# A two-layer GLA and MLA trunk on Trainium2: first products from a transposed copy of x, its norm applied afterwards, c_q in 512-column blocks

## The chip, the cores and the metric

The kernel runs on one core of a Trainium2 chip. The metric is the device time of one execution in microseconds (us). The engines are TensorE (PE in the profile; its weight loads are PEld), VectorE (DVE), ScalarE (ACT), GpSimd (POOL) and SyncE (SP), which issues most of the DMA transfers. Each runs its own instructions in a fixed order and waits on semaphores for the others.

## The reference

One sequence of 512 rows of width 2048 goes through two layers; each takes an RMS norm of x, a token mixer, an RMS norm of the mixer's output, and adds it to x. All in float32. Cut to what matters here:

```python
def rms_norm(x, g, eps=1e-6):
    return x * rsqrt(mean(x * x, -1) + eps) * g

for i in range(2):
    h = rms_norm(x, g_pre)
    y = gla_mixer(h, ...) if i == 0 else mla_mixer(h, ...)
    x = x + rms_norm(y, g_post)

def gla_mixer(h, ...):            # 4 heads, 256 wide in q and k, 512 in v
    q, k, v, gate, gk_low = split(h @ w_in)      # 1024, 1024, 2048, 2048, 16
    log_a = log_sigmoid(gk_low @ w_gk2 + b_gk) / 16
    ...                           # chunked linear attention with decays from log_a
    return (rms_norm(o, g_onorm) * silu(gate)) @ w_out

def mla_mixer(h, ...):            # 16 heads
    c_q, c_kv, k_rope, gate = split(h @ w_in)    # 512, 512, 64, 2048
    q  = rms_norm(c_q,  g_qa)  @ w_qb
    kv = rms_norm(c_kv, g_kva) @ w_kvb
    ...                           # causal softmax attention
    return (o * silu(gate)) @ w_out
```

## The kernel before

**Products.** Every large product is made of three matmuls (`mm3`, L123): each factor is split into a high part, which the fast matmul format holds exactly, and the rest (`act_hi`, `act_lo`; `w_hi`, `w_lo`), and hi x hi, hi x lo and lo x hi are added up in a PSUM bank. `act_hi` and `act_lo` hold the normed x transposed, as 16 slices k of 128 rows by 512 columns. Weights come in chunks: SyncE loads half a megabyte (`chunk_load`, three buffers), ScalarE writes the high part and VectorE the rest (`chunk_split`, four buffers). Where a norm's gain g belongs in front of the product, `chunk_split` multiplies it into the weights, one k at a time (L118, L119); without a gain it takes the whole chunk in one copy and one subtraction (L110, L111). `block_s` makes products with the sequence on the rows of the result (four row tiles s, four banks), `block_t` with the sequence on the columns.

**The start** (`start`, L224). x is loaded by rows, 1 MB for each row tile s, the first in four pieces. For each s ScalarE sums the squares, `rstd_of` makes the factor, and `rows_to_act` (L324) scales the rows, has PE transpose them in 16 blocks of 128x128 (L333, four to a bank) and splits the result into `act_hi` and `act_lo`. In between PE makes the products of v for head 0, columns 0 to 255, with 4 k to a chunk. The gains of the norm before layer 0 arrive as rows and are transposed by PE (`gain_t`), other gains likewise later (`gcols` in `constants`). Then `gla` makes columns 256 to 511 of v (L346), the 16 columns of gk_low with 48 columns of weights (`gk_low`), and for each head the q/k block, the gate block, v, scores and values. Evacuations: `v_evac` splits v, `qk_block` multiplies q and k by their decays, `silu` makes the gate.

**Between the layers** (`between`, L611, called by `out_proj` for each s when the last columns are done). VectorE adds the residual to `yo` in four passes (L619), ScalarE sums squares, SyncE stores the new x (`x1d`), and `rows_to_act` norms and transposes it for layer 1, as at the start. `cq_ahead` (L688) has loaded and split the weights of columns 0 to 255 of c_q for 14 of the 16 k before. `mla` then makes, s by s, columns 0 to 255 of c_q from these, and columns 256 to 511 by `block_s`, 4 k to a chunk; `latent_evac` norms the rows of c_q, and `latent_end` transposes them (`lat_t`).

**What sets the order.** The code is written once in program order; a scheduler then fixes the order of instructions on each engine, and in that order each engine waits. PE's order thus interleaves transposes with products. Transposes use two PSUM banks (`pt`), products four, and two are left for scores.

Of the kernel before, what the change touches and what calls it, by code (L numbers as in the profile page):

```python
# [70 lines left out]
class Trunk:  # L71
# [152 lines left out]
    def start(self):  # L224

        nc, a, cp = self.nc, self.a, self.cp
        xs = a["x"][0]
        xt = [self.slot(f"g{s}", [P, D], F32, f"x{s}") for s in range(ST)]
        rows = self.tmp([KT, P], F32, "gain_rows")
# [1 line left out]
        for g in range(4):
            c = slice(g * 512, (g + 1) * 512)
            nc.sync.dma_start(xt[0][:, c], xs[0:P, c])
            if g == 0:
                nc.scalar.dma_start(cf, a["consts"])
                nc.scalar.dma_start(rows, a["l0_pre_norm"].rearrange("(r c) -> r c", c=P))
# [5 lines left out]
        nc.tensor.transpose(pt[:, 0:KT], rows, self.ident[0:KT, 0:KT])
        self.g_in = cp.tile([P, KT], F32, name="g_in0")
        nc.vector.tensor_copy(self.g_in, pt[:, 0:KT])
        w = a["l0_gla_w_in"]
        load = lambda i: self.chunk_load(w, 4 * i, 4, [(GV0, 256)])
        raws = [load(0)]
        nc.sync.dma_start(xt[1], xs[P:2 * P, :])
        raws.append(load(1))
        nc.sync.dma_start(xt[2], xs[2 * P:3 * P, :])  # L250
        raws.append(load(2))
        ws = []
        self.v_ps = [self.acc(f"v_acc{s}", s == 3) for s in range(ST)]
        for s in range(ST):
            parts = self.st.tile([P, 4], F32, tag="parts", name="parts", bufs=2)
            for g in range(4):
                self.sumsq(xt[s][:, g * 512:(g + 1) * 512], parts[:, g:g + 1])
            rstd = self.rstd_of(self.total(parts, "x_ssq"), D, "x_rstd")
            self.rows_to_act(s, xt[s], rstd)
            for i in range(4):  # L260
                if s == 0:
                    if i == 3:
                        raws.append(load(3))
                        nc.sync.dma_start(xt[3], xs[3 * P:4 * P, :])
                    ws.append(self.chunk_split(raws[i], 4 * i, self.g_in, hi_on=nc.vector if i % 2 else None))
                self.part_s(s, 4 * i, ws[i], self.v_ps, slice(0, 256), self.act_hi, self.act_lo, KT)

    def constants(self):
# [21 lines left out]
        pt = self.pst.tile([P, 512], F32, tag="pt", name="gcols")  # L290
        nc.tensor.transpose(pt[:, 0:NROWS], rows[0:NROWS, :], self.ident[0:NROWS, 0:NROWS])
        self.gcol = cp.tile([P, NROWS], F32, name="gcol")
        nc.vector.tensor_copy(self.gcol, pt[:, 0:NROWS])
        with self.tc.issue_after(self.last_norm.ins):
# [635 lines left out]
```

## Time and profile before

| | us |
|---|---|
| median of 3 runs | 1505.87 (1505.53 to 1507.59) |
| the profiled execution | 1507.5 |
| its span in the profile | 1505.7 |
| PE busy in it | 1485.8 (99%) |
| DVE, ACT busy | 742.5 (49%), 657.1 (44%) |
| DMA, mean | 100 GB/s |

The span runs from the first instruction to the last; times in timelines are counted from its start. PE's busy time is pipelined: two matmuls overlap, so what one costs in a row of them is the distance of their starts, not the duration beside it. PE is busy in all 40 slices of the page but for the first and the last; so the order of its instructions and what it waits for there are what a reader has to look at.

### The profile page before, as it was taken

Reading aid. Unit: us, or ns where it says so; the run is one execution under the profiler, and the core shown is the slowest. Engines: PE = TensorE matmul, PEld = TensorE weight load, DVE = VectorE, ACT = ScalarE, POOL = GpSimd, SP = SyncE. Lnnn points to the kernel's source line nnn. Section 1 sums busy time; section 2 is a strip of 40 time slices with the busy share of each in tenths; the row PEclk is TensorE's granted clock in tenths of the full one; section 3 lists DMA queues with packets and bytes.
Section 4 is the critical chain, followed back from the end, with each engine's and each line's share of the span. In section 5 each row is a group of like instructions: output and inputs, shape, how many; then the busy total and the mean of one; then the engine's idle time right before and its main releaser. Section 6 shows DMA issues by size and latency. Waiting matters only on the chain.

```text
span 1505.7 us, 19208 instructions
## 1 busy us (share of the span) xinstructions
PE 1485.8 (99%) x7490; PEld 1266.6 (84%) x7490; DVE 742.5 (49%) x1337; ACT 657.1 (44%) x1250; POOL 35.0 (2%) x72
## 2 busy tenths in 40 slices
PE   7999999999999999999999999999999999999998
PEld 6988888888888888888889888888888899888886
DVE  6544653355436445434355443333577677853234
ACT  6542642254225424333244443344566667742221
POOL 2100000000000000100011000000000000000000
PEclk9999999999999999999999999999999999999999
DMA  6423223322331323434252333333222111234223
GB/s 222 122 71 98 71 87 95 101 82 80 90 110 57 98 84 119 134 111 134 91 188 92 101 98 98 98 99 91 74 74 74 50 50 55 83 126 168 98 91 119
DMA packets 113867, 149.91 MB, mean 100 GB/s; under 512 B 17580, under 2 KB 66976, under 8 KB 112368
## 3 DMA queue, kind: packets, MB, share of 16 engines
q1 hardware_dynamic: 110176, 136.86, 29.9%
q0 software_dynamic: 3424, 11.75, 2.4%
q8 instruction: 58, 0.95, 0.3%
q14 instruction: 33, 0.27, 0.1%
q10 hardware_dynamic: 176, 0.07, 0.0%
HBM read 140.08 MB, written 8.59 MB: 99 GB/s over the span
## 4 chain that ended last, share of the span: by engine, by line
PE 95%; DVE 2%; ACT 1%; DMA 1%; issue 0%; SPq 0%; DVEq 0%; ACTq 0%
PE acc L125 11%; PE acc L127 11%; PE acc L126 11%; PE yo_acc L125 8%; PE yo_acc L126 8%; PE yo_acc L127 8%; PE v_acc L127 5%; PE v_acc L125 5%; PE v_acc L126 5%; PE o_t L127 1%; PE o_t L126 1%; PE q_acc L127 1%; PE q_acc L126 1%; PE q_acc L125 1%; PE o_t L125 1%; PE pt L882 1%
## 5 line engine op out<-in xcount | busy, mean ns | idle before, releaser
L125 PE MATMUL acc<-act_hi,w_hi 128*128 128x512 f32 x768 | 299.7, 390 | 0.0
L126 PE MATMUL acc<-act_hi,w_lo 128*128 128x512 f32 x768 | 299.2, 390 | 0.0
L127 PE MATMUL acc<-act_lo,w_hi 128*128 128x512 f32 x768 | 298.9, 391 | 0.0
L119 DVE SCALAR_TENSOR_TENSOR w_lo<-w_raw,g_in,w_hi 128x512 fp32r<-128x512 f32 (+1 forms) x208 | 139.7, 707 | 206.7 <-ACT w_hi L118 206.6
L118 ACT ACTIVATE w_hi<-w_raw,g_in 128x512 fp32r<-128x512 f32 (+1 forms) x200 | 128.1, 689 | 242.9 <-PE acc L127 166.6
L127 PEld LDWEIGHTS acc<-act_lo,w_hi 128*128 128x128 f32 x768 | 144.2, 188 | 30.7 <-issue 0.7
L125 PEld LDWEIGHTS acc<-act_hi,w_hi 128*128 128x128 f32 x768 | 144.2, 188 | 30.4 <-issue 0.7
L126 PEld LDWEIGHTS acc<-act_hi,w_lo 128*128 128x128 f32 x768 | 144.3, 188 | 29.8
L111 DVE TENSOR_TENSOR w_lo<-w_raw,w_hi 128x1024 fp32r<-128x1024 f32 x64 | 78.4, 1225 | 166.7 <-ACT w_hi L110 166.6
L110 ACT CAST w_hi<-w_raw 128x1024 fp32r<-128x1024 f32 x64 | 67.3, 1051 | 168.4 <-PE yo_acc L126 156.8
L125 PE MATMUL yo_acc<-w_hi,act_hi 128*128 128x512 f32 x352 | 137.5, 391 | 0.0
L126 PE MATMUL yo_acc<-w_hi,act_lo 128*128 128x512 f32 x352 | 137.1, 390 | 0.0
L127 PE MATMUL yo_acc<-w_lo,act_hi 128*128 128x512 f32 x352 | 137.1, 391 | 0.0
L119 DVE SCALAR_TENSOR_TENSOR w_lo<-w_raw,gcol,w_hi 128x512 fp32r<-128x512 f32 (+1 forms) x98 | 64.6, 699 | 106.1 <-ACT w_hi L118 105.9
L126 PE MATMUL v_acc<-w_hi,act_lo 128*128 128x512 f32 (+1 forms) x320 | 112.2, 352 | 0.0
L118 ACT ACTIVATE w_hi<-w_raw,gcol 128x512 fp32r<-128x512 f32 (+1 forms) x98 | 61.4, 677 | 115.5 <-PE acc L127 83.8
L125 PE MATMUL v_acc<-w_hi,act_hi 128*128 128x512 f32 (+1 forms) x320 | 111.5, 351 | 0.2 <-ACT act_hi L174 0.2
L127 PE MATMUL v_acc<-w_lo,act_hi 128*128 128x512 f32 (+1 forms) x320 | 110.7, 350 | 0.0
L127 PEld LDWEIGHTS yo_acc<-w_lo,act_hi 128*128 128x128 f32 x352 | 66.1, 188 | 14.0 <-issue 0.2
L125 PEld LDWEIGHTS yo_acc<-w_hi,act_hi 128*128 128x128 f32 x352 | 66.1, 188 | 13.8 <-issue 0.2
L126 PEld LDWEIGHTS yo_acc<-w_hi,act_lo 128*128 128x128 f32 x352 | 66.1, 188 | 13.4
L125 PEld LDWEIGHTS v_acc<-w_hi,act_hi 128*128 128x128 f32 x320 | 61.4, 192 | 8.0 <-ACT act_hi L174 0.6
(300 smaller groups left out, 2688.9 us busy)
## 6 DMA issues: line engine op xcount, KB each, us to landing
w_raw<-in_l_gla_w_in_dram SPq DMA_DIRECT2D x64, 512.0 KB, 3.7
w_raw<-in_l_mla_w_in_dram SPq DMA_DIRECT2D x47, 512.0 KB, 3.7
w_raw<-in_l_gla_w_in_dram SPq DMA_DIRECT2D x64, 256.0 KB, 3.0
w_raw<-in_l_gla_w_out_dram SPq DMA_DIRECT2D x32, 512.0 KB, 3.7
w_raw<-in_l_mla_w_out_dram SPq DMA_DIRECT2D x32, 512.0 KB, 3.6
pw_raw<-in_l_mla_w_kvb_dram SPq DMA_DIRECT2D x64, 128.0 KB, 2.3
xo<-in_x_dram POOLq DMA_DIRECT2D x16, 256.0 KB, 6.0
x1d<-yo SPq DMA_DIRECT2D x4, 1024.0 KB, 5.8
```

The lines of the kernel that those rows point to most:

```text
L110: nc.scalar.copy(hi, raw)
L111: nc.vector.tensor_tensor(lo, raw, hi.bitcast(F32), ALU.subtract)
L118: nc.scalar.activation(hi[:, kk, :], raw[:, kk, :], AF.Copy, scale=g)
L119: nc.vector.scalar_tensor_tensor(lo[:, kk, :], raw[:, kk, :], g, hi[:, kk, :].bitcast(F32), ALU.mult, ALU.subtract)
L125: t.matmul(out, lh, rh, start=start, stop=False)
L126: t.matmul(out, ll, rh, start=False, stop=False)
L127: t.matmul(out, lh, rl, start=False, stop=stop)
L882: te.transpose(pt[:, o:o + P], probs[i][:, j * P:(j + 1) * P], self.ident)
```

## The change

- x is also given transposed by the host (`xt`), and all gains as columns of one table (`gains`, 52 columns; `gcol`). The two PE transposes of gains go.
- `start` loads x^T in slices k, two at a time, alternating with weight chunks of 2 k by 512 columns of v. `x_split` writes `act_hi` and `act_lo` of a slice from x^T times the gain of layer 0, without the norm's factor: the 64 transposes of x go. The v block of head 0 is made of 512 columns at once; its chunks need no gain.
- The squares of x are summed per slice on ScalarE (`x_sq`) and VectorE (`x_ssq`, 128x512); before the last two k, `x_norm` sums them over partitions by matmuls with ones and makes the factor twice: as a column for each s (`rcol`) and along the sequence on all partitions (`rrow`).
- The factor is applied to the products: `v_evac` scales by `rcol`; the q/k blocks, the gates and gk_low are multiplied by `rrow` on VectorE. Weights of layer 0 are split without a gain.
- The weights of gk_low are prepared inside the v loop (`gk_weights`).
- c_q is made of 512 columns: `cq_ahead` prepares 7 of 16 k by 512 columns, `mla` adds the eighth, and `block_s` makes k 8 to 15 for all 512 columns.

```diff
     def start(self):
...
+        xs = [self.slot(f"g{i}", [P, 4, S], F32, f"xt{i}") for i in range(4)]
+
+        def load_x(k0, nk):
+            nc.sync.dma_start(xs[k0 // 4][:, k0 % 4:k0 % 4 + nk, :],
+                              a["xt"][k0 * P:(k0 + nk) * P, :].rearrange("(k p) n -> p k n", p=P))
+
+        self.gcol = cp.tile([P, NCOLS], F32, name="gcol")
+        nc.scalar.dma_start(self.gcol, a["gains"])
+        load_x(0, 1)
+        raws = [self.wp.tile([P, 2, 512], F32, tag="raw", name="w_raw", bufs=3)]
+        for k in range(2):
+            nc.sync.dma_start(raws[0][:, k, :], w[k * P:(k + 1) * P, GV0:GV0 + 512])
+            if k == 0:
+                load_x(1, 1)
...
+        for k0 in range(0, KT, 2):
+            if k0:
+                load_x(k0, 2)
+                raws.append(self.chunk_load(w, k0, 2, [(GV0, 512)]))
+            x = xs[k0 // 4][:, k0 % 4:k0 % 4 + 2, :]
+            if k0:
+                self.x_split(k0, 2, x)
+                wt = self.chunk_split(raws[-1])
+            else:
...
+                for k in range(2):
+                    self.x_split(k, 1, x[:, k:k + 1, :])
+                    v.tensor_copy(hi[:, k, :], raws[0][:, k, :])
+                    v.tensor_tensor(lo[:, k, :], raws[0][:, k, :], hi[:, k, :].bitcast(F32), ALU.subtract)
...
+                    nc.scalar.activation(sq, x[:, i, :], AF.Square)
+                    v.tensor_tensor(ssq, ssq, sq, ALU.add)
+            if k0 == 10:
+                self.gk_weights()
+            if k0 + 2 == KT:
+                self.x_norm(ssq)
+            for s in range(ST):
+                if k0 + 2 == KT:
+                    with self.tc.issue_after(self.norm_mm.ins):
+                        self.part_s(s, k0, wt, ps, slice(0, 512), self.act_hi, self.act_lo, KT)
+                    self.v_evac(s, ps[s])
+                else:
+                    self.part_s(s, k0, wt, ps, slice(0, 512), self.act_hi, self.act_lo, KT)
+
+    def x_split(self, k0, nk, x):
...
+            self.nc.scalar.activation(self.act_hi[:, k, :], x[:, i, :], AF.Copy, scale=g)
+            self.nc.vector.scalar_tensor_tensor(self.act_lo[:, k, :], x[:, i, :], g,
+                                                self.act_hi[:, k, :].bitcast(F32),
+                                                ALU.mult, ALU.subtract)
+
+    def x_norm(self, ssq):
...
         for s in range(ST):
...
+            nc.tensor.matmul(pc[:, s:s + 1], ssq[:, s * P:(s + 1) * P], self.ones[:, 0:1],
+                             start=True, stop=True)
+        pn = self.pss.tile([P, 512], F32, tag="sc", name="x_norm")
+        self.norm_mm = nc.tensor.matmul(pn, self.ones, ssq, start=True, stop=True)
...
     def v_evac(self, s, ps):
-        self.split_from(ps, self.vh[s], self.vl[s])
+        r = self.rcol[:, s:s + 1]
+        self.last_evac = self.nc.scalar.activation(self.vh[s], ps, AF.Copy, scale=r)
+        self.nc.vector.scalar_tensor_tensor(self.vl[s], ps, r, self.vh[s].bitcast(F32),
+                                            ALU.mult, ALU.subtract)
...
         def evac(t, ps):
             d = t % 2
+            n = self.tmp([P, S], F32, "qk")
+            v.tensor_tensor(n, ps, self.rrow, ALU.mult)
...
-    def silu(self, out, ps):
+    def silu(self, out, ps, r=None):
...
+        if r is not None:
+            nc.vector.tensor_tensor(g, ps, r, ALU.mult)
+            ps = g
...
-        self.cq_w.append(self.chunk(w, KT - 2, 2, [(MQ0, 256)], self.g_in))
+        self.cq_w.append(self.chunk(w, KT // 2 - 1, 1, [(MQ0, 512)], self.g_in))
         for s in range(ST):
             for i, wt in enumerate(self.cq_w):
-                self.part_s(s, 2 * i, wt, ps, slice(0, 256), hi, lo, KT)
-        self.block_s(w, MQ0 + 256, 256, 256, ps, hi, lo, KT, evac=self.latent_evac, gain=self.g_in)
+                self.part_s(s, i, wt, ps, slice(0, 512), hi, lo, KT)
+        self.block_s(w, MQ0, 512, 0, ps, hi, lo, KT, evac=self.latent_evac, gain=self.g_in,
+                     ks=(KT // 2, KT))
...
-        for k0, nk in ((0, 4), (4, 4), (8, 4), (12, 2)):
-            raw = self.chunk_load(w, k0, nk, [(MQ0, 256)])
...
+        for k0, nk in ((0, 2), (2, 2), (4, 2), (6, 1)):
+            raw = self.chunk_load(w, k0, nk, [(MQ0, 512)])
```

How the scheduler's order moves is seen at three places. First PE at the start of the program. Before:

```order
L242 MATMUL gain_t<-cf,gain_rows 128x16
L333 MATMUL xn_t<-cf,xn 128x128 x8
L125 MATMUL v_acc_109<-w_hi,act_hi 128x256
L333 MATMUL xn_t<-cf,xn 128x128 x4
L126 MATMUL v_acc_109<-w_hi,act_lo 128x256
L127 MATMUL v_acc_109<-w_lo,act_hi 128x256
```

Now:

```order
L125 MATMUL v_acc_101<-w_hi,act_hi 128x512
L125 MATMUL v_acc_102<-w_hi,act_hi 128x512
L125 MATMUL v_acc_103<-w_hi,act_hi 128x512
L125 MATMUL v_acc_104<-w_hi,act_hi 128x512
L126 MATMUL v_acc_101<-w_hi,act_lo 128x512
L126 MATMUL v_acc_102<-w_hi,act_lo 128x512
```

The transposes (`xn_t`) are gone, and PE goes through the four row tiles (`v_acc_101` to `104`) for each slice k, instead of through the k of one row tile.

Second ScalarE in the first tens of microseconds, where it prepares x and the weights of the v block (`xt_82` to `xt_85` hold k 0 to 3, 4 to 7, 8 to 11, 12 to 15; before, `x_84` is a row tile). Before:

```order
L118 ACTIVATE w_hi<-w_raw,g_in_99 128x256 x4
L174 CAST act_hi<-xn_t 128x4x128 x2
L185 ACTIVATE junk,parts<-x_83 128x512 x4
L174 CAST act_hi<-xn_t 128x4x128
L180 ACTIVATE x_rstd<-x_ssq,eps 128x1
L185 ACTIVATE junk,parts<-x_84 128x512
```

Now, from the cast of the weights of k 4 and 5 to that of k 6 and 7:

```order
L110 CAST w_hi<-w_raw 128x1024
L294 ACTIVATE act_hi<-xt_83,gcol 128x512 x2
L275 ACTIVATE x_sq<-xt_83 128x512 x2
L294 ACTIVATE act_hi<-xt_84,gcol 128x512 x2
L275 ACTIVATE x_sq<-xt_84 128x512 x2
L294 ACTIVATE act_hi<-xt_84,gcol 128x512 x2
L275 ACTIVATE x_sq<-xt_84 128x512 x2
L294 ACTIVATE act_hi<-xt_85,gcol 128x512 x2
L110 CAST w_hi<-w_raw 128x1024
```

Copies and squares of x up to k = 13 stand ahead of the cast of the weights of k 6 and 7.

Third VectorE between the layers (`yo_5040` and `yo_4570` are row tile 2, `yo_5049` and `yo_4579` row tile 3). Before:

```order
L581 TENSOR_TENSOR yo_5049<-yo_acc_5557,gain 128x512
L330 TENSOR_SCALAR xn<-yo_5040,x_rstd 128x512 x4
L619 SCALAR_TENSOR_TENSOR yo_5049<-yo_5049,y_rstd,xo 128x512 x4
L175 TENSOR_TENSOR act_lo<-xn_t,act_hi 128x4x128 x2
L189 TENSOR_REDUCE x_ssq<-parts 128x1
```

Now:

```order
L625 TENSOR_TENSOR yo_4579<-yo_acc_5073,gain 128x512
L175 TENSOR_TENSOR act_lo<-xn_t,act_hi 128x4x128
L366 TENSOR_SCALAR xn<-yo_4570,x_rstd 128x512 x4
L663 SCALAR_TENSOR_TENSOR yo_4579<-yo_4579,y_rstd,xo 128x512 x4
L175 TENSOR_TENSOR act_lo<-xn_t,act_hi 128x4x128 x2
L189 TENSOR_REDUCE x_ssq<-parts 128x1
```

The splits of the transposed row tile 2 still stand behind the four passes over row tile 3; on PE, 138 matmuls of 256 columns stood between the first c_q matmul and the third group of transposes of row tile 2, and 85 of 512 columns now.

## Rows read from the trace of the kernel before

**Rows 1.** Waits of PE, whole span: engine, line, releaser, total us, times, longest

```profile
PE xn_t L333 <- DVE xn L330: 4.1, 1, 4.1
PE xn_t L333 <- DVE act_lo L175: 2.9, 3, 2.0
```

**Rows 2.** Timeline of PE, start: start us, us, engine, line, out<-in, idle before

```profile
9.57 1.97 PE L333 MATMUL xn_t<-cf,xn 128*128 128x128 f32 x8 [4.15 <-DVE xn L330]
...
13.71 0.56 PE L126 MATMUL v_acc<-w_hi,act_lo 128*128 128x256 f32 x1
...
18.33 0.41 PE L125 MATMUL v_acc<-w_hi,act_hi 128*128 128x256 f32 x1
18.54 0.36 PE L126 MATMUL v_acc<-w_hi,act_lo 128*128 128x256 f32 x1
...
30.82 0.28 PE L127 MATMUL v_acc<-w_lo,act_hi 128*128 128x256 f32 x1
30.94 0.60 PE L333 MATMUL xn_t<-cf,xn 128*128 128x128 f32 x4
...
31.50 0.60 PE L333 MATMUL xn_t<-cf,xn 128*128 128x128 f32 x4
```

**Rows 3.** Timeline of PE, from the second half of v to the q/k block

```profile
46.71 0.28 PE L125 MATMUL v_acc<-w_hi,act_hi 128*128 128x256 f32 x1
...
68.91 0.39 PE L393 MATMUL gkl_acc<-act_hi,gkl_w 128*48 128x512 f32 x1
...
76.29 0.40 PE L125 MATMUL acc<-act_hi,w_hi 128*128 128x512 f32 x1
...
83.33 0.39 PE L127 MATMUL acc<-act_lo,w_hi 128*128 128x512 f32 x1
```

**Rows 4.** Timeline of PE in the c_q block

```profile
784.26 0.28 PE L125 MATMUL cq_acc<-cqw_hi,act_hi 128*128 128x256 f32 x1
...
802.32 0.66 PE L333 MATMUL xn_t<-cf,xn 128*128 128x128 f32 x4 [1.96 <-DVE act_lo L175]
...
840.36 0.38 PE L718 MATMUL lat_t<-cf,lat_row 128*128 128x128 f32 x2
```

**Rows 5.** Windows: PE, PEld, DVE, ACT, POOL busy us (count), PE clock, DMA share, GB/s

```profile
805.00:806.00 1.00, 1.00 (x7) 1.00 (x6) 0.81 (x3) 0.30 (x1) 0.00 (x0) 0.50 0.01 0
```

**Rows 6.** DMA issues, whole span: out<-in, queue, count, KB each, us to landing

```profile
w_raw<-in_l_gla_w_in_dram SPq DMA_DIRECT2D x64, 512.0 KB, 3.7
...
gain_rows<-in_l_pre_norm_dram ACTq DMA_DIRECT2D x1, 8.0 KB, 3.8
```

**Rows 7.** Timeline of ACT, start, where it waits for loads

```profile
4.52 0.63 ACT L185 ACTIVATE junk<-x 128x512 bf16<-128x512 f32 x1 [2.50 <-DMA x<-in_x_dram]
...
6.76 0.63 ACT L185 ACTIVATE junk<-x 128x512 bf16<-128x512 f32 x1 [0.68 <-DMA x<-in_x_dram]
...
9.50 1.71 ACT L118 ACTIVATE w_hi<-w_raw,g_in 128x256 fp32r<-128x256 f32 x4 [0.51 <-DMA w_raw<-in_l_gla_w_in_dram]
```

**Rows 8.** Groups by shape, ACT and DVE: busy us, mean ns, idle before

```profile
L118 ACT ACTIVATE w_hi<-w_raw,g_in 128x512 fp32r<-128x512 f32 x176 | 117.9, 716 | 239.6 <-PE acc L127 166.6 <-PE v_acc L126 62.7 <-issue 10.3
L110 ACT CAST w_hi<-w_raw 128x1024 fp32r<-128x1024 f32 x64 | 67.3, 1051 | 168.4 <-PE yo_acc L126 156.8 <-PE v_acc L126 4.3 <-DMA w_raw<-in_l_mla_w_out_dram 3.1
...
L545 ACT ACTIVATE o_sq<-o_t 128x512 f32<-128x512 f32 x12 | 7.1, 596 | 20.7 <-PE o_t L127 20.7
...
L546 DVE TENSOR_TENSOR o_ssq<-o_ssq,o_sq 128x512 f32<-128x512 f32 x12 | 8.3, 690 | 16.6 <-ACT o_sq L545 16.6
```

**Rows 9.** Timeline of PE around the norm of one head's output

```profile
202.13 1.02 PE L549 MATMUL o_norm<-o_ssq,ones 128*128 128x512 f32 x2
...
203.22 0.39 PE L125 MATMUL acc<-act_hi,w_hi 128*128 128x512 f32 x1
```

**Rows 10.** Windows, as rows 5, in the start

```profile
10.00:15.00 5.00, 4.18 (x19) 3.49 (x18) 4.34 (x12) 4.24 (x12) 0.00 (x0) 1.00 1.04 370
```

More of the change, by code (lines that the diff above doesn't have):

```diff
@@ L224, in start @@
     def start(self):
[L226 to L229, printed above, removed]
-        cf = cp.tile([P, P + 1], F32, name="cf")
[L231 to L236, printed above, removed]
+        nc, v, a, cp = self.nc, self.nc.vector, self.a, self.cp
@@ L242, in start @@
[L242 to L253, printed above, removed]
@@ L254, in start @@
-        for s in range(ST):
[L255 to L266, printed above, removed]
+        self.ones = cp.tile([P, P], F32, name="ones")
@@ new lines, in x_split @@
+    def x_split(self, k0, nk, x):
+        for i in range(nk):
+            k = k0 + i
+            g = self.gcol[:, R_IN + k:R_IN + k + 1]
+            self.nc.scalar.activation(self.act_hi[:, k, :], x[:, i, :], AF.Copy, scale=g)
[3 more added lines that the diff above has]
+    def x_norm(self, ssq):
+        nc = self.nc
+        pc = self.pss.tile([P, 512], F32, tag="sc", name="x_norm_c")
+        for s in range(ST):
+            nc.tensor.matmul(pc[:, s:s + 1], ssq[:, s * P:(s + 1) * P], self.ones[:, 0:1],
+                             start=True, stop=True)
+        pn = self.pss.tile([P, 512], F32, tag="sc", name="x_norm")
+        self.norm_mm = nc.tensor.matmul(pn, self.ones, ssq, start=True, stop=True)
+        self.rcol = self.st.tile([P, ST], F32, tag="rcol", name="rcol", bufs=1)
+        self.rrow = self.slot("b25", [P, S], F32, "rrow")
+        nc.scalar.activation(self.rcol, pc[:, 0:ST], AF.Ln, scale=1.0 / D, bias=self.eps)
+        nc.scalar.activation(self.rcol, self.rcol, AF.Exp, scale=-0.5)
+        nc.scalar.activation(self.rrow, pn, AF.Ln, scale=1.0 / D, bias=self.eps)
+        self.last_norm = nc.scalar.activation(self.rrow, self.rrow, AF.Exp, scale=-0.5)
@@ L289, in constants @@
         self.big = big.to_broadcast([P, P])
[L290 to L294, printed above, removed]
+        with self.tc.issue_after(self.last_evac.ins):
             self.trig(posi, self.invf)
@@ L356, in gla @@
                 self.v_begin()
-                self.block_s(w, GV0 + h * GDV, 512, 0, ps, hi, lo, KT, evac=self.v_evac, gain=self.g_in)
+                self.block_s(w, GV0 + h * GDV, 512, 0, ps, hi, lo, KT, evac=self.v_evac)
             else:
@@ L910, in _constants, with _laid_out @@
     return {"consts": cf, "masks": masks}
+def _laid_out(given):
+    names = ("l0_gla_b_gk", "l0_gla_g_onorm", "l1_mla_g_qa", "l1_mla_g_kva", "l1_pre_norm", "l0_pre_norm")
+    rows = np.concatenate([given[n].reshape(-1, P) for n in names])
+    return {"xt": np.ascontiguousarray(given["x"][0].T), "gains": np.ascontiguousarray(rows.T)}
 def kernel(**inputs):
@@ L920 @@
     given.update(_constants())
+    given.update(_laid_out(given))
     arrays, a = {}, {}
```

79 lines of the change are left out of this document (42 added, 37 removed).

## The prediction, made before the changed kernel was run

> **What bounds the kernel now.** TensorE does. The first view is the list of what PE waits for: over the whole span its matmul side sits idle for a few microseconds only, nearly all of it in two places, the first microseconds and one spot near 800 us [rows 1]. So a change gains by what it takes off PE's own stream, or off those two places; what it takes off or adds to VectorE and ScalarE counts only where PE waits for them. The second view is PE's timeline. At the start PE has no real work until 9.57 us: x is loaded, squared, summed, normed and then transposed by PE itself in groups of four [rows 2]. The last pace at 1.2 GHz is seen at 18.33 to 18.54 (0.21 us for 256 columns); by 30.82 to 30.94 the same matmul takes 0.12, which is 2.4 GHz [rows 2]. The third view is the same timeline further on, where nothing waits and start-to-start times are prices [rows 3]. The fourth is the spot at 800 us, where PE stops for 1.96 us [rows 4] and the granted clock then shows 0.50, the 1.2 GHz level [rows 5].
>
> **Prices.** 256 columns: 185 matmuls from 46.71 to 68.91, 22.20/185 = 0.120 us. 512 columns: 31 from 76.29 to 83.33, 7.04/31 = 0.227 us [rows 3]. Two narrow ones cost 0.240, so a wide one saves 0.013. A group of four transposes: from 30.82 to 31.50 lie one group and two matmuls of 0.12, so 0.44 us [rows 2].
>
> **The start, part by part.** The place to compare is the first matmul of the q/k block, at 76.29 us before [rows 3]. It waits for nothing in either kernel: v_evac frees the accumulators of the v block while PE is in gkl_acc (7.38 us, 68.91 to 76.29), so what PE finishes earlier there is kept.
>
> The new start removes from PE: the wait until 9.57; 16 groups of transposes, 16 x 0.44 = 7.0 us; 384 narrow matmuls for 192 wide ones, 192 x 0.013 = 2.5 us; the waits between the first groups; and the gcols transpose. Rather than subtract, I build the new time up.
>
> - First matmul. It needs gcol, the first slice of x^T, the first slice of w, an act_hi and a w_hi. gcol is a small load like gain_rows, 3.8 us from issue to landing [rows 6], issued at about 0.8, so 4.6. The first quarter megabyte of x was in use at 4.52 before, and the third was waited for until 6.76 [rows 7]; the new queue has x, w, x, w in quarters, so w's first comes second, between the two, about 5.6. Then a Square (0.60) and a scaled copy (0.72) on ScalarE from 4.52 give 5.8, and a cast on VectorE gives 6.1. I take **6.1 us**; the bounds are 5.8 and 7.5 (w as late as the third piece).
> - The half pace. Before, it lasted from the first transposes at 9.57, or from the dense matmuls from 13.71 on, until 18.54 [rows 2]: 4.8 to 9 us. The new stream is dense from its first matmul, as the old one from 13.71, so I take the near end, 5 us, which does 2.5 us of work: **2.5 us** lost (bound 4.5).
> - 192 x 0.227 = **43.6 us**.
> - One wait. The scheduler puts on ScalarE, ahead of the cast of the weights of k = 6, 7, the copies of x for k = 6 to 13 and their squares (second pair of order pieces). Counted from 4.52: 12 squares x 0.60, 14 scaled copies x 0.72 and three casts x 1.05 [rows 8] are 20.4 us; two landings hold it up, x's k = 1 (6.76 against 5.8) and k = 2, 3, which end at 1.5 MB of the queue as the first w_raw before did, at 9.50 (against 8.1) [rows 7]: 2.4 us. So these weights are ready at 27.3. PE wants them at 6.1 + 2.5 + 72 x 0.227 = 24.9. Durations overlap a little back to back, so I take **2 us** (bounds 0 and 4). From there on ScalarE is ahead: a pair of k costs it 1.44 + 1.2 + 1.05 = 3.7 us against PE's 24 x 0.227 = 5.45.
> - The norm. x_norm is one fp32 matmul of 512 columns: as o_norm, 202.13 to 203.22 less the one matmul inside, 0.86 us [rows 9]. x_norm_c is four with one column and full weights; not seen before. As eight passes at the 0.11 of a transpose, 0.9; as eight at 0.43, 3.5; I take the transpose, whose weight load is the same: **1.7 us** together. Their input is long there, since the last squares run some 10 us earlier. The Ln/Exp chain and v_evac hide behind the last 24 matmuls (5.4 us) and gkl_acc.
> - gkl_acc, unchanged: **7.4 us**.
>
> Sum 6.1 + 2.5 + 43.6 + 2.0 + 1.7 + 7.4 = 63.3 against 76.3: **13.0 us gained**.
>
> **Between start and end of layer 0.** rrow adds a product of 0.69 [rows 8] to each of 16 q/k tiles and 16 gate tiles, 22 us on VectorE; the splits without a gain give some of it back, and PE does not wait for either here. It would if a bank were freed late, but the product is the first and only reader of the bank. Zero; the cover is that PE is three weight chunks behind its suppliers. If each of the 32 were exposed it would be 22 us, and nothing excludes a few.
>
> **The c_q block.** Before: from the first cq matmul at 784.26 to the first lat_t at 840.36, 56.1 us [rows 4]. Work in it: 384 x 0.120 = 46.1 and 14 groups x 0.44 = 6.2, together 52.3. The missing 3.8 us are the stop at 800.09 to 802.32 (2.2 less 0.12) and the half clock after it, about 1.7. The stop: PE is in order and wants the third group of transposes of rows s = 2, whose bank is released by an act_lo that stands on VectorE behind four passes over yo of s = 3 (third pair of order pieces). That order is the same afterwards. But PE arrives later: 138 narrow matmuls lay between the first cq matmul and that group, 16.6 us, and now 85 wide ones, 19.3 us, so 2.7 us later than before, against a stop of 2.1. VectorE is also a little earlier, since seven wide splits replace fourteen narrow ones. So stop and half clock go. Next in line are the weights of k = 12, 13, loaded behind two stores of x1d as the third narrow chunk was; PE comes to them at about 794, and the old chunk's split ended about then: I leave 0.5 us for that and for lat_t. New: 192 x 0.227 + 6.2 + 0.5 = 50.3, **5.8 us gained** (bounds 2, when stop and half clock stay, and 6.4).
>
> **Sum.** 13.0 + 5.8 = 18.8. The profiled execution took 1507.5 us (span 1505.7 and 1.8 around it): 1488.7. The median of the runs shown, 1505.87, is 1.6 lower: **1487**.
>
> **Rivals.**
> 1. The start is starved. Either the wait at k = 6 lets the clock fall, as after the 1.96 us at 802, which cost 1.7 us beyond the stop, or landings come later than in the old queue and the wait doubles: +1.7 to +6, 1489 to 1493. For it: the wait is as long as the one that did it [rows 4, 5]. Against: the half clock may come or not after so short a stop. [...]
> 2. The stop at 800 stays, because VectorE is late by more than the 2.7 us that PE gained: +3.8, 1491. Together with rival 1, up to 1496.
> 3. Slower. The queue no longer overlaps its pieces, which are 0.25 to 0.5 MB where three were 1 MB. A half megabyte alone takes 3.7 us to land [rows 6]; one after another a pair of k needs 7.4 us for x and w against 5.45 of PE work, PE stops 2 us in every pair, and the clock stays at half: 192 x 0.454 = 87 us instead of 48, +39 - 19 = +20, 1526. It decides from some 83 matmuls of the 192 at half pace (83 x 0.227 = 18.8). Against it: 370 GB/s between 10 and 15 us with pieces of both sizes in flight [rows 10]; 8.4 MB at that rate are 23 us, half of PE's 48. The rule that speaks against the change is in the Trainium skill, "DMA: Bandwidth & Descriptors", Bandwidth: "Batch DMAs to ≥1 MiB for ≥75% of peak." By that page's fit for one DMA a half megabyte is an estimated 3.2 us, close to the row's 3.7, and sixteen in single file would feed PE until about 52 us; the sum would be near 1493. The measured rate says that they do not go in single file.
> 4. The change not doing what it says: the order shows the transposes gone and the blocks wide, so only the saving per wide matmul could fail, 5 us in all, 1492.
>
> **How the numbers follow.** Forecast (1484 to 1489) 0.52; rival 1 alone 0.22; rival 2 alone 0.10; both 0.08; rival 4 0.02; better than the forecast 0.03; rival 3 0.03. The range 1483 to 1496 leaves out rival 3 and some of the edges, and holds the bounds of the first matmul (+1.4), of the wait (-2, +2) and of the small matmuls (+2.6), which do not all fall on one side. A measurement of this kernel tells 0.2% (3 us) from no change. Faster by more than that: 0.95; within: 0.02; slower: 0.03.
>
> **What would show it.** In the new profile: the first v_acc matmul near 6 us; the pace turning from 0.43 to 0.227 near 11; a wait on w_hi near 25, of some 2 us, and none after it; the first q/k matmul near 63; no wait near 790 and the clock at 1.00 through the c_q block; first cq to first lat_t 50 us. Wrong would be a wait on a DMA landing in each pair (rival 3), 0.50 in the clock after 25 us (rival 1), a wait for act_lo in the c_q block (rival 2), or PE waiting for a product with rrow between 63 and 750 us, for which I have allowed nothing.

## The result and the profile after

| | before | after |
|---|---|---|
| median, us | 1505.87 (5 runs, 1505.53 to 1507.76) | 1490.05 (5 runs, 1489.52 to 1490.32) |
| ratio | | 0.9891, 95% interval 0.9876 to 0.9905 |
| the profiled execution, its span | 1507.5, 1505.7 | 1490.05, 1488.3 |
| PE busy | 1485.8 | 1472.6 |
| DVE, ACT busy | 742.5, 657.1 | 738.0, 625.7 |

The change makes the kernel 15.8 us faster by the medians, and the forecast of 1487 was 3 us too low. The program before has executions of two lengths: of 31 timed with the first experiments 26 have spans of 1503.3 to 1504.9 and five of 1505.6 to 1506.5, and the profiled one (1505.7) is of the longer kind. So the spans of the two traces differ by 17.4 us and the medians by 15.8. This matters below. Two disturbed runs, one of the kernel before (2129.5 us) and one of an experiment (3320.0 us), are left out of all medians and counts.

What PE waits for in the kernel after, the whole span (engine, line, releaser, total us, times, longest), which answers to [rows 1]:

```profile
PE v_acc L125 <- DVE w_hi L267: 6.4, 1, 6.4
PE lat_t L763 <- DVE lat_row L755: 0.7, 1, 0.7
PE cq_acc L125 <- ACT act_hi L174: 0.5, 1, 0.5
PE k_acc L125 <- DVE qr_t L863: 0.3, 1, 0.3
PE v_acc L127 <- DVE w_lo L111: 0.2, 1, 0.2
PE v_acc L125 <- ACT w_hi L110: 0.2, 1, 0.2
```

The 4.1 us for `xn` and the stop of 2.0 us on `act_lo` are gone. What is left is the time to the first product and five small waits: two in the start (`w_hi` and `w_lo` of k = 6, 7), one that was there before (`qr_t`), and two new ones in the c_q block (`lat_row` and `act_hi`).

PE's timeline of the kernel after (start us, us, engine, line, out<-in, idle before), which answers to [rows 2, 3]:

```profile
6.37 2.04 PE L125 MATMUL v_acc<-w_hi,act_hi 128*128 128x512 f32 x4 [6.37 <-DVE w_hi L267]
...
11.54 1.09 PE L125 MATMUL v_acc<-w_hi,act_hi 128*128 128x512 f32 x4
12.46 1.09 PE L126 MATMUL v_acc<-w_hi,act_lo 128*128 128x512 f32 x4
...
24.95 0.39 PE L127 MATMUL v_acc<-w_lo,act_hi 128*128 128x512 f32 x1
25.49 0.50 PE L125 MATMUL v_acc<-w_hi,act_hi 128*128 128x512 f32 x1 [0.15 <-ACT w_hi L110]
...
47.91 0.94 PE L304 MATMUL x_norm_c<-ones,x_ssq 128*128 128x1 f32 x8
48.71 1.10 PE L307 MATMUL x_norm<-x_ssq,ones 128*128 128x512 f32 x2
49.25 0.80 PE L125 MATMUL v_acc<-w_hi,act_hi 128*128 128x512 f32 x1
...
55.14 0.40 PE L431 MATMUL gkl_acc<-act_hi,gkl_w 128*48 128x512 f32 x1
...
62.52 0.40 PE L125 MATMUL acc<-act_hi,w_hi 128*128 128x512 f32 x1
```

No transposes stand there. The first 12 products go at 0.43 us (6.37 to 11.54), four take 0.92 from 11.54 to 12.46, 0.23 each, and the q/k block begins at 62.52 instead of 76.29 [rows 3]: 13.8 us earlier. At k = 6 PE is held for 0.3 us.

The c_q block of the kernel after, on the same timeline, which answers to [rows 4]:

```profile
770.54 0.39 PE L125 MATMUL cq_acc<-cqw_hi,act_hi 128*128 128x512 f32 x1
...
781.04 0.50 PE L125 MATMUL cq_acc<-cqw_hi,act_hi 128*128 128x512 f32 x1 [0.49 <-ACT act_hi L174]
...
821.36 0.39 PE L127 MATMUL cq_acc<-w_lo,act_hi 128*128 128x512 f32 x1
822.48 0.41 PE L763 MATMUL lat_t<-cf,lat_row 128*128 128x128 f32 x2 [0.73 <-DVE lat_row L755]
```

It begins 13.7 us earlier than before, so layer 0 has lost nothing of the start's gain; and it lasts 51.9 us instead of 56.1. The granted clock is 1.00 throughout it. The first `lat_t` is 17.9 us earlier than before, the last matmul 17.8 (1480.46 against 1498.21), the span 17.4.

### The profile page after: what moved, and what is told of

It reads as the page before. It is cut to its first block, busy times and chain, and to the rows that moved or that the text cites. A ratio compares the mean times of both kernels' runs of the same rounds, so it can differ in the third digit from the quotient of the medians.

```text
span 1488.3 us, 18065 instructions
## 1 busy us (share of the span) xinstructions
PE 1472.6 (99%) x7050; PEld 1235.8 (83%) x7050; DVE 738.0 (50%) x1229; ACT 625.7 (42%) x1109; POOL 32.5 (2%) x67
## 4 chain that ended last, share of the span: by engine, by line
PE 95%; DMA 2%; DVE 1%; ACT 1%; issue 1%; SPq 0%; DVEq 0%; ACTq 0%
PE acc L127 11%; PE acc L126 11%; PE acc L125 11%; PE yo_acc L125 8%; PE yo_acc L127 8%; PE yo_acc L126 8%; PE v_acc L127 5%; PE v_acc L126 5%; PE v_acc L125 5%; PE o_t L126 1%; PE o_t L127 1%; PE q_acc L126 1%; PE q_acc L127 1%; PE q_acc L125 1%; PE o_t L125 1%; PE pt L927 1%
## 5 line engine op out<-in xcount | busy, mean ns | idle before, releaser
L111 DVE TENSOR_TENSOR w_lo<-w_raw,w_hi 128x1024 fp32r<-128x1024 f32 x159 | 194.4, 1223 | 379.9 <-ACT w_hi L110 379.5
L110 ACT CAST w_hi<-w_raw 128x1024 fp32r<-128x1024 f32 x159 | 167.3, 1053 | 429.1 <-PE acc L127 186.7
L119 DVE SCALAR_TENSOR_TENSOR w_lo<-w_raw,gcol,w_hi 128x512 fp32r<-128x512 f32 x89 | 63.2, 747 | 101.1 <-ACT w_hi L118 101.0
L118 ACT ACTIVATE w_hi<-w_raw,gcol 128x512 fp32r<-128x512 f32 x89 | 59.8, 716 | 112.0 <-PE acc L127 83.8
L125 PE MATMUL v_acc<-w_hi,act_hi 128*128 128x512 f32 x256 | 100.1, 395 | 6.5 <-DVE w_hi L267 6.4
L126 PE MATMUL v_acc<-w_hi,act_lo 128*128 128x512 f32 x256 | 99.5, 393 | 0.0
L127 PE MATMUL v_acc<-w_lo,act_hi 128*128 128x512 f32 x256 | 97.0, 393 | 0.2 <-DVE w_lo L111 0.2
L126 PEld LDWEIGHTS yo_acc<-w_hi,act_lo 128*128 128x128 f32 x352 | 66.1, 188 | 13.7
L125 PEld LDWEIGHTS yo_acc<-w_hi,act_hi 128*128 128x128 f32 x352 | 66.1, 188 | 13.7 <-issue 0.2
L125 PEld LDWEIGHTS v_acc<-w_hi,act_hi 128*128 128x128 f32 x256 | 48.6, 190 | 17.2 <-issue 6.3
L126 PE MATMUL yo_acc<-w_hi,y_lo 128*128 128x512 f32 x160 | 62.5, 391 | 0.0
L125 PE MATMUL yo_acc<-w_hi,y_hi 128*128 128x512 f32 x160 | 62.4, 391 | 0.0
```

The costliest lines, as they stand in the source:

```text
L110: nc.scalar.copy(hi, raw)
L111: nc.vector.tensor_tensor(lo, raw, hi.bitcast(F32), ALU.subtract)
L118: nc.scalar.activation(hi[:, kk, :], raw[:, kk, :], AF.Copy, scale=g)
L119: nc.vector.scalar_tensor_tensor(lo[:, kk, :], raw[:, kk, :], g, hi[:, kk, :].bitcast(F32), ALU.mult, ALU.subtract)
L125: t.matmul(out, lh, rh, start=start, stop=False)
L126: t.matmul(out, ll, rh, start=False, stop=False)
```

## The experiments

Medians of 4 to 11 runs; each ratio is to the kernel before, timed alongside. It took 1506.19 to 1506.24 there, 0.3 us more than with the result, so a difference of that size to the changed kernel's 1490.05 says nothing. A further run of the kernel before tells what the two lengths are.

**The kernel before, again.**

> The kernel before, once more, for its spread. The times known so far fall in two places, near 1505.5 and near 1507.6 us; the profiled execution was of the second kind and had granted clock 0.50 for 3.4 us after the stop in the c_q block, which costs 1.7. Theory: the two kinds differ by just this; an execution of 1507.6 shows 0.50 near 804 to 807 us, one of 1505.5 shows 1.00 there and first cq to first lat_t in 54.4 instead of 56.1. Rival: they differ in the start (first q/k matmul at 74 instead of 76.3), and the c_q block takes 56.1 in both.

Measured: 1505.98 (ratio 1.0002, 0.9993 to 1.0011). The profiled execution was again of the longer kind (span 1506.4; three of its eleven are above 1506): `xn_t` waits 2.05 us, then the clock (columns as in [rows 5]):

```profile
804.00:805.00 1.00, 1.00 (x6) 1.00 (x6) 0.59 (x1) 0.77 (x3) 0.00 (x0) 0.50 0.97 393
805.00:806.00 1.00, 1.00 (x7) 1.00 (x6) 1.00 (x4) 0.00 (x0) 0.00 (x0) 0.50 0.64 262
```

The first q/k matmul at 76.6 and the block of 56.5 us are those of the first trace. No execution of the shorter kind was profiled, so that it lacks the 0.50 is not shown; the next experiment bears on it.

**Each part alone.** `start_only` has `mla` and `cq_ahead` of before:

```diff
-        self.cq_w.append(self.chunk(w, KT // 2 - 1, 1, [(MQ0, 512)], self.g_in))
+        self.cq_w.append(self.chunk(w, KT - 2, 2, [(MQ0, 256)], self.g_in))
...
-        for k0, nk in ((0, 2), (2, 2), (4, 2), (6, 1)):
-            raw = self.chunk_load(w, k0, nk, [(MQ0, 512)])
+        for k0, nk in ((0, 4), (4, 4), (8, 4), (12, 2)):
+            raw = self.chunk_load(w, k0, nk, [(MQ0, 256)])
```

> The changed kernel with the c_q block put back to 256 columns (and weights prepared for 14 k of 256). Theory, that the two parts add up: first q/k matmul at 62.5 as in the changed kernel; the stop on act_lo (2.0 us) and the 0.50 clock after it are there again; first cq to first lat_t 56.1 (54.4 without the half clock); median 1490.05 + 2.5 to 4.2 = 1492.5 to 1494.2. Rival, that the stop only hung on the times at which the old start put things: no stop, c_q 52.3 to 53, median 1490.5 to 1491.

> The kernel before with only the c_q block made of 512 columns. Theory, that the two parts add up: first q/k matmul at 76.3 as before; no stop of the transposes and no 0.50 clock; first cq to first lat_t 51.9; median 1505.87 less 2.5 to 4.2 = 1501.7 to 1503.4. Rival, that wide blocks alone leave the stop: 1503.5 to 1505, with a wait for act_lo of 1 us or more.

Measured: `start_only` 1492.45 (0.9916, 0.9902 to 0.9930), `cq_only` (the same edit the other way round, in the kernel before) 1503.04 (0.9980, 0.9971 to 0.9990). The parts add up: 1505.98 less 13.5 for the start and 2.9 for c_q is 1489.5, against 1490.05. The stop in the block is there with 256 columns and gone with 512. PE's timeline of `start_only`, and its clock after the stop:

```profile
788.15 0.66 PE L369 MATMUL xn_t<-cf,xn 128*128 128x128 f32 x4 [1.30 <-DVE act_lo L175]
```

```profile
790.00:791.00 1.00, 1.00 (x11) 1.00 (x11) 1.00 (x4) 0.29 (x1) 0.00 (x0) 1.00 0.76 311
```

Here PE waited 1.30 us and the clock stayed at 1.00; the block took 53.9 us. Of its five runs two were 1.6 and 2.6 us longer. So in the ordinary execution c_q gains 2.4 to 2.9 us, not the 4.2 of the two traces: the difference is about the 1.7 us of half clock, as it would be if only the longer kind pays it. What `cq_only` waits for in the block is `lat_row`, as after (0.8 us).

**The width of the first v block.** Each product of 512 columns cut in two:

```diff
-                    self.part_s(s, k0, wt, ps, slice(0, 512), self.act_hi, self.act_lo, KT)
+                    self.part_n(s, k0, wt, ps)
...
+            for j in range(2):
+                c = slice(j * 256, (j + 1) * 256)
+                self.mm3(ps[s][:, c], self.act_hi[:, k, r], self.act_lo[:, k, r],
+                         w[0][:, kk, c], w[1][:, kk, c], k == 0 and j == 0, k == KT - 1 and j == 1)
```

> The changed kernel with each 512-column matmul of the first v block cut into two of 256. Theory, that a wide one saves 0.013 us against two narrow ones here too: first q/k matmul 192 x 0.013 = 2.5 us later, at 65.0, median 1492.5. Rival, that the block is bound by its supply of x and weights and the width gives nothing: 62.5 and 1490.

Measured: first q/k matmul at 65.11, 2.6 us later; median 1492.88 (0.9912, 0.9898 to 0.9926), 2.8 more. The narrow products go at 0.120 us there, so the 0.013 per wide matmul holds; the total is less clean, since the first product is 0.3 us later and a wait for `w_lo` grows to 1.04.

**The transposes put back.** Four groups before the products of each of k = 6, 8, 10, 12:

```diff
+            for g in range(4 if 6 <= k0 <= 12 else 0):
+                pt = self.pst.tile([P, 512], F32, tag="pt", name="again_t")
+                for j in range(4):
+                    nc.tensor.transpose(pt[:, j * P:(j + 1) * P], x[:, g // 2, j * P:(j + 1) * P], self.ident)
```

> The changed kernel with the 16 groups of four transposes of x put back on PE, between the products of the first v block from k = 6 on; nothing reads them. Theory: 16 x 0.44 = 7.0 us, less the 0.7 us that PE waits at k = 6 and 7 in the changed kernel: first q/k matmul at 68.8 to 69.5, median 1496.4 to 1497.1. Rival, that the groups overlap with the products around them or were hidden behind the supply of weights: 66 or less, under 1494.

Measured: first q/k matmul at 68.76, median 1496.68 (0.9933, 0.9920 to 0.9947), 6.6 more. One group on PE's timeline there:

```profile
39.61 0.60 PE L284 MATMUL again_t<-cf,xt 128*128 128x128 f32 x4
39.96 0.48 PE L125 MATMUL v_acc<-w_hi,act_hi 128*128 128x512 f32 x1
40.28 0.39 PE L126 MATMUL v_acc<-w_hi,act_lo 128*128 128x512 f32 x1
```

From 39.61 to 40.28 lie the group and one product of 0.23, so 0.44 us, the price read before. Nearly half of the start's gain is what these groups cost, 6.6 us here.

**The products with rrow, twice.**

```diff
-            v.tensor_tensor(n, ps, self.rrow, ALU.mult)
+            for _ in range(2):
+                v.tensor_tensor(n, ps, self.rrow, ALU.mult)
```

and the same in `silu`.

> The changed kernel with each of the 32 products with rrow on VectorE made twice. Theory, that they lie beside PE's work: 32 x 0.69 = 22 us more on VectorE, and first q/k to first c_q as in the changed kernel, 708.0 us; 1490.1. Rival, that what was gained in the start is partly lost again behind these products: at least the one that releases the bank for the next block is on the path in each of 8 blocks, 5.5 us, 1495.6; all of them exposed 22 us, 1512.

Measured: 1489.78 (0.9888, 0.9874 to 0.9901), the same as the changed kernel. Its groups on VectorE (busy us, mean ns, idle before) and two rows of PE:

```profile
L521 DVE TENSOR_TENSOR gate<-acc,rrow 128x512 f32<-128x512 f32 x32 | 20.1, 680 | 0.0
L504 DVE TENSOR_TENSOR qk<-acc,rrow 128x512 f32<-128x512 f32 x32 | 20.1, 679 | 0.0
```

```profile
62.58 0.40 PE L125 MATMUL acc<-act_hi,w_hi 128*128 128x512 f32 x1
...
770.58 0.39 PE L125 MATMUL cq_acc<-cqw_hi,act_hi 128*128 128x512 f32 x1
```

Twice as many products with `rrow` lie beside PE's work, and from the first q/k to the first c_q it is 708.0 us, as in the changed kernel (708.02). VectorE's half of the span that is free covers them.

**What the half pace at the start costs.** Products of zeros ahead of the first:

```diff
+        v.memset(self.junk, 0.0)
+        warm = self.pss.tile([P, 512], F32, tag="sc", name="warm")
+        for i in range(11):
+            nc.tensor.matmul(warm, self.junk[:, 0:P], self.junk, start=True, stop=True)
```

> The changed kernel with 11 matmuls of 512 columns on a tile of zeros put ahead of the first product, in the 6 us in which PE has nothing to do; nothing reads them. Theory: the pace is 0.227 from the first product on or soon after it, which is 2.5 us of half pace less, but hardly any of it reaches the end, since PE then waits for the cast of the weights of k = 2, 3 (done at 13.2) and again for that of k = 6, 7 (25.4): first q/k matmul at 62.2 to 62.5, 1489.8. Rival 1, that the half pace alone sets the end of the block: 60.0, 1487.6. Rival 2, that work on zeros does not raise the clock: pace 0.43 until 11.4, no new wait, 1490.1.

Measured: 1489.87 (0.9892, 0.9879 to 0.9906). PE's timeline and the two rows of ScalarE behind it:

```profile
4.61 1.24 PE L252 MATMUL warm<-junk 128*128 128x512 bf16 x3
6.30 1.17 PE L125 MATMUL v_acc<-w_hi,act_hi 128*128 128x512 f32 x4 [0.46 <-DVE w_hi L271]
7.31 1.07 PE L126 MATMUL v_acc<-w_hi,act_lo 128*128 128x512 f32 x4
...
13.50 0.50 PE L125 MATMUL v_acc<-w_hi,act_hi 128*128 128x512 f32 x1 [1.49 <-ACT w_hi L110]
...
25.70 0.50 PE L125 MATMUL v_acc<-w_hi,act_hi 128*128 128x512 f32 x1 [1.02 <-ACT w_hi L110]
...
62.74 0.40 PE L125 MATMUL acc<-act_hi,w_hi 128*128 128x512 f32 x1
```

```profile
12.41 1.03 ACT L110 CAST w_hi<-w_raw 128x1024 fp32r<-128x1024 f32 x1
...
24.62 1.03 ACT L110 CAST w_hi<-w_raw 128x1024 fp32r<-128x1024 f32 x1
```

The pace is 0.25 and then 0.23 from the first product on, and nothing clear of the noise reaches the end (0.2 us less in the median, the first q/k matmul 0.2 later): PE is earlier and waits for the casts of k = 2, 3 and of k = 6, 7. Up to k = 7 the supply sets the time and the half pace is free. On this row the Trainium skill bears, "TensorE: Matmul & The Clock Gate", Part 1: activity releases the half rate. By the pace the trace agrees, 0.25 us behind 11 products of zeros against 0.43 without them. The clock column doesn't show it: in the changed kernel it reads 1.00 over the products at 0.43 too, so in these first microseconds only the pace tells. The changed kernel's row (columns as in [rows 5]):

```profile
6.00:11.00 5.00, 4.63 (x11) 3.69 (x12) 4.10 (x8) 2.32 (x4) 0.00 (x0) 1.00 1.05 333
```

**ScalarE pair by pair**, alone and with the products of zeros:

```diff
+                with after(cast):
+                    self.x_split(k0, 2, x)
...
+                cast = nc.scalar.copy(wt[0], raws[-1])
...
+                        with self.tc.issue_after(cast.ins):
+                            nc.scalar.activation(sq, x[:, i, :], AF.Square)
```

> The changed kernel with ScalarE going pair by pair: copies of x for a pair of k, cast of its weights, squares; so the cast of k = 6, 7 stands at about 18 us instead of 24.4. Theory: the two waits at k = 6 and 7 (0.3 and 0.4 us) go and nothing else: first q/k matmul at 61.8, 1489.4. Rival, that the waits are replaced by one at k = 2 or by a late sum of squares in front of x_norm: 62.5 or later, 1490 to 1492.

> Both: matmuls on zeros ahead of the first product, and ScalarE pair by pair. Theory: now the 2.5 us of half pace reach the end less a wait at k = 2, whose weights are cast at about 12.1 while PE comes at 11.8: first q/k matmul at 59.3 to 59.8, 1486.9 to 1487.4. Rival, that the supply of the first pairs sets the end whatever PE's pace: 61.8, 1489.4.

Measured: `early_cast` 1488.95 (0.9884, 0.9871 to 0.9898; its four runs spread over 2.5 us), first q/k matmul at 61.63; `warm_early` 1487.56 (0.9876, 0.9862 to 0.9889), at 59.67. Timeline of `warm_early`, PE and ScalarE:

```profile
12.31 0.50 PE L125 MATMUL v_acc<-w_hi,act_hi 128*128 128x512 f32 x1 [0.29 <-ACT w_hi L270]
...
59.67 0.40 PE L125 MATMUL acc<-act_hi,w_hi 128*128 128x512 f32 x1
```

```profile
20.69 1.05 ACT L270 CAST w_hi<-w_raw 128x1024 fp32r<-128x1024 f32 x1 [2.94 <-DMA w_raw<-in_l_gla_w_in_dram]
```

Only with the order changed is the pace worth something: 2.0 us at the first q/k matmul, 1.4 between the two medians. One number was off: the cast of k = 6, 7 moved to 20.69 (21.20 in `early_cast`), not to 18, since now it waits for its landing. `warm_early` is the fastest kernel of this study; `warm_pe`, in the same series, took 2.3 us more.

**A later cast.**

```diff
+                if k0 == 6:
+                    for _ in range(8):
+                        last = nc.scalar.activation(self.junk, x[:, 0, :], AF.Square)
+                    with self.tc.issue_after(last.ins):
+                        wt = self.chunk_split(raws[-1])
```

> The changed kernel with three squares of x more on ScalarE (written to a scrap tile) and one of the others moved, all ahead of the cast of the weights of k = 6, 7: 4 x 0.52 = 2.1 us more before it. Theory, that PE's arrival at k = 6 is pinned to this cast (in the changed kernel it waits there by 0.3 us): all 2.1 us reach the end, first q/k matmul at 64.6, 1492.1, if the pace stays at 0.227 after the wait; 1493.8 if the granted clock falls to 0.50 after it as it did in the c_q block before. Rival, that there is slack: 62.5, 1490.

Measured: 1498.15 (0.9947, 0.9933 to 0.9960). The kernel that ran has eight squares more, not the three of the expectation, and the cast ends at 34.65 instead of 25.44. The scheduler also moved `x_norm` up on PE, behind k = 5, where it waits for all squares of x. ScalarE's cast, PE's steps around it, and the clock:

```profile
33.62 1.03 ACT L110 CAST w_hi<-w_raw 128x1024 fp32r<-128x1024 f32 x1
```

```profile
31.44 1.83 PE L310 MATMUL x_norm_c<-ones,x_ssq 128*128 128x1 f32 x8 [6.42 <-DVE x_ssq L282]
...
34.70 0.92 PE L125 MATMUL v_acc<-w_hi,act_hi 128*128 128x512 f32 x1
```

```profile
28.00:29.00 1.00, 0.00 (x0) 0.00 (x0) 1.00 (x2) 1.00 (x3) 1.00 (x3) 0.50 0.06 17
...
38.00:39.00 1.00, 1.00 (x6) 0.83 (x5) 1.00 (x3) 0.24 (x1) 0.00 (x0) 0.92 0.99 360
```

The first product of k = 6 starts at 34.70, where the cast has just ended and `x_norm` has just gone through PE, so the run does not tell which of the two held it: by the cast alone PE would have stood until the same 34.7 (an estimate). That is 9.2 us later than in the changed kernel. The half pace from 34.7 to 38.2 costs 1.75 more; `x_norm` (1.75) and the wait at 27.21 (0.4) are no longer paid behind it. Together this is 8.8 us, and the first q/k matmul comes 8.6 us later, at 71.08. What 2.1 us at the cast cost was not measured; that a stop can be paid once more in clock was.

**x loaded twice.**

```diff
+                for k in (k0, k0 + 1):
+                    t = self.slot(f"b{(8 + k - 2) if k < 14 else k + 8}", [P, S], F32, "x_again")
+                    nc.sync.dma_start(t, a["xt"][k * P:(k + 1) * P, :])
```

> The changed kernel with the slices of x from k = 2 on loaded a second time on the same queue, behind the first (3.7 MB more beside 8.4 MB, in 14 pieces of a quarter megabyte; nothing reads them). Theory, that the pieces overlap and the start has bandwidth to spare: at 385 GB/s the weights of k = 6, 7, behind 3 MB more, land 7.8 us later, at about 25 instead of 17, so their cast begins at 25 to 26 instead of 24.4; first q/k matmul at 63.1 to 64.5, median 1490.6 to 1492. Rival, that pieces go in single file at 2.6 us for a quarter and 3.7 us for half a megabyte: PE waits for a landing in each pair, and 14 x 2.6 us more in the queue put the first q/k matmul at 85 or later, 1512 or more.

Measured: 1491.40 (0.9901, 0.9884 to 0.9917); the first q/k matmul of the profiled execution, at 65.43, lies behind the expected 64.5. The pieces do not go in single file (columns as in [rows 5]):

```profile
20.00:26.00 6.00, 6.00 (x29) 4.95 (x28) 5.67 (x8) 5.04 (x9) 1.52 (x2) 1.00 1.05 387
```

In the profiled execution PE waits once, 2.07 us at 32.75, for the cast of k = 8, 9, which this order puts late, and not at k = 6; the clock is 0.50 from 33.7 to 37.1, and the span of 1491.0 is 1.3 to 2.1 us above those of the other three runs. These spans would fit a program that does or does not lose its clock after a stop of some 2 us, here too; no trace of the shorter ones shows it. Rival 3 is refuted. The Trainium skill's rule to batch to 1 MiB ("DMA: Bandwidth & Descriptors", Bandwidth) is in this kernel no reason against the change: pieces of 0.25 and 0.5 MB moved 387 GB/s.

**Everything earlier.** On top of `warm_early`:

```diff
-        nc.scalar.dma_start(self.gcol, a["gains"])
...
+        for k, q in ((0, nc.scalar), (1, nc.sync)):
+            q.dma_start(raws[0][:, k, :], w[k * P:(k + 1) * P, GV0:GV0 + 512])
+            if k == 0:
+                nc.scalar.dma_start(self.gcol, a["gains"])
```

with 7 products of zeros, `cf` and w_gk2 loaded later, and `latent_end` of c_q called behind the first chunk of the next block.

> Matmuls on zeros ahead (7), ScalarE pair by pair, and besides: the first piece of w on ScalarE's queue beside the first of x, copies of x ahead of the first squares, the table cf and the weights w_gk2 loaded after the first pairs, and the transposes of c_q behind the first matmuls of the next block. Theory: first product at about 4.4 instead of 6.3; PE then waits some 1.4 us for the weights of k = 2, 3; first q/k matmul at 58.1 to 58.9; no wait for lat_row, which gives 0.9; median 1485.1 to 1486.2. Rival, that the landing of k = 2, 3 does not move, at 10 us: the wait there grows by what the first product gained, first q/k at 59.7, median 1486.6.

Measured: 1489.62 (0.9889, 0.9875 to 0.9902); both theories fall. ScalarE's timeline and PE's:

```profile
6.75 1.33 ACT L315 ACTIVATE act_hi<-xt,gcol 128x512 fp32r<-128x512 f32 x2 [4.74 <-DMA gcol<-in_gains_dram]
```

```profile
7.53 1.88 PE L125 MATMUL v_acc<-w_hi,act_hi 128*128 128x512 f32 x4 [3.14 <-ACT act_hi L315]
```

The 26 KB of gains, now second in ScalarE's queue behind a quarter of a megabyte of w, arrive at 6.75, so the first product is late by 1.2 us; the products of zeros had ended 3 us earlier, and the granted clock is back at 0.50 from 7.8 to 11.2. The first piece of w was cast at 5.53 against 5.75: another queue hardly brings it earlier. And the first product of the next block waits for `lat_row` instead of `lat_t` (1.0 us), since it needs the bank that `lat_row` reads.

## Why the prediction held, by its steps

**Start: 13.0 forecast, 13.8 measured.** The terms:

| term | forecast | in the trace after |
|---|---|---|
| first product | 6.1 | 6.37, w cast on VectorE at 5.80 |
| half pace | 2.5 | 2.45 (12 products in 5.17 us) |
| 192 products | 43.6 | 43.6 at 0.227 |
| wait at k = 6, 7 | 2.0 | 0.7 (0.3 at 24.95, 0.4 at 27.21) |
| norm | 1.7 | 1.75 (1.34 from 47.91, and 0.41 behind it) |
| gkl_acc | 7.4 | 7.38 |
| sum | 63.3 | 62.25, measured 62.52 |

The wait was sized from durations; in a row the steps of ScalarE are closer. Its timeline after:

```profile
13.14 1.33 ACT L294 ACTIVATE act_hi<-xt,gcol 128x512 fp32r<-128x512 f32 x2
14.38 1.14 ACT L275 ACTIVATE x_sq<-xt 128x512 f32<-128x512 f32 x2
15.43 1.04 ACT L110 CAST w_hi<-w_raw 128x1024 fp32r<-128x1024 f32 x1
16.36 1.34 ACT L294 ACTIVATE act_hi<-xt,gcol 128x512 fp32r<-128x512 f32 x2
```

Start to start a copy is 0.62, a square 0.53, a cast 0.93, where I took 0.72, 0.60 and 1.05: 2.7 us less over the 29 steps, against a somewhat later landing of k = 2, 3 (9.92). PE's prices had been taken start to start, ScalarE's not. The sum also treats the half pace and this wait as terms that add, and they are alternatives: `warm_pe` took 2.45 from the one, and the waits at k = 2 to 7 took all of it (0.7 to 3.2 us). Had the sum put the first product at 4.5, it would have come out 1.6 us lower, and by these waits the kernel would not have.

**Layer 0: 0 forecast, 0 measured**, and `rrow_twice` shows that 22 us more would still lie beside PE.

**The c_q block: 5.8 forecast, 4.2 between the traces, 2.4 to 2.9 in the medians.** Width and transposes, 49.8 us, were right (`start_only` and `cq_only`: the stop is gone with the wide block). The step that failed in size is "I leave 0.5 us for that and for lat_t". It was 2.1: the two new waits stretch PE's steps by 0.65 at 780.16 and 0.89 at 821.36, and 0.6 lies in small pieces. The wait for `lat_row` comes with the wide block (`start_only` has none): in the last chunk a row tile now ends every 4 products, 0.91 us, where 12 narrow ones took 1.44, while ScalarE needs 0.9 us for the sum of squares and factor of a tile. Before the first of these it splits the next block's weights, which in this trace landed late; how much of the wait is theirs was not tested. ScalarE after:

```profile
818.64 1.34 ACT L118 ACTIVATE w_hi<-w_raw,gcol 128x512 fp32r<-128x512 f32 x2 [2.55 <-DMA w_raw<-in_l_mla_w_in_dram]
819.89 0.57 ACT L185 ACTIVATE junk<-cq_acc 128x512 bf16<-128x512 f32 x1
```

This wait is in every kernel with the wide block; that for `act_hi` only in some. The wide blocks took 50.9 to 52.8 us (without `combined`, which moves `lat_t`).

That the `act_lo` stop goes because PE arrives later was the mechanism, and it held, but the 2.7 us came out by luck: the groups were counted wrongly. The group that stopped is not the third of row tile 2 but the first; the two `act_lo` behind the four passes, of which one frees its bank, are row tile 1's and not row tile 2's. By PE's timelines 109 narrow products lay before it and 67 wide ones do now, not 138 and 85: 13.1 and 15.2 us, 2.1 later. The new wait for `act_hi` adds its 0.65. PE and VectorE after:

```profile
789.38 0.60 PE L369 MATMUL xn_t<-cf,xn 128*128 128x128 f32 x4
```

```profile
788.04 1.28 DVE L175 TENSOR_TENSOR act_lo<-xn_t,act_hi 128x512 fp32r<-128x512 f32 x2
```

The first of the two `act_lo` ends at 788.68 and PE comes at 789.38: 0.7 us to spare. In `cq_only`, which has no wait for `act_hi`, it is 0.7 too (801.69 and 802.39).

**The last subtraction.** "The median of the runs shown, 1505.87, is 1.6 lower" took 1.6 us off after the stop's half clock, 1.7, had been counted as a gain. Both are the same thing, if the shorter executions before lack the 0.50: the block's gain in the medians, 2.4 to 2.9 against 4.2, and `start_only` without 0.50 speak for it, but no trace of a short execution of before shows it. Without the double count the forecast is 1488.7; the rest to 1490.05 is -0.8 in the start, +1.6 in the c_q block, and 0.5 behind it and around the span, where the cause was not followed.

**The rivals.** 1 (0.22): no; the wait was 0.7 us and the clock stayed at 1.00 from 11.4 us on; but its price is real, as `late_cast` shows. 2 (0.10): no, there is no wait for `act_lo`. 3 and 4: refuted by `x_twice` and `narrow_v`. The time fell 1 us above the forecast's own range and into that of rival 1, but through small new waits elsewhere and the double count; that it stayed so near the forecast is in part luck, since the start gained 0.8 us more than forecast where c_q gained 1.6 less.

## What to carry to other kernels

Where two limits take turns, as supply and pace do in a start, relieving one only uncovers the other: ask of each stage who is late, and change both. Take prices of every engine start to start, not from durations. And when the profiled execution is longer than the median, find what in it is unusual before its stops are counted as gains.

## What was not expected of the hardware

A stop of PE is not always followed by half clock: after waits of 1.30 (`start_only`) and of 1.49 and 1.02 us (`warm_pe`) the granted clock stayed at 1.00, after 1.96 to 3.14 (the two of the kernel before, `x_twice`, `combined`) it was 0.50 for 3.4 us in the profiled executions. By their spans other executions of the same programs may have been spared; none of those was profiled. And the 26 KB of gains, behind a quarter of a megabyte in ScalarE's queue, took until 6.75 us, where first in that queue they were in use by 3.94.
